# Full-height products for the first block's logits, and two sets of tensors by way of DRAM

## The chip, the cores and the metric

The kernel runs on one core of one Trainium2 chip. The metric is the device time of one launch in microseconds. Of the kernel before, three runs gave 2621.33, 2624.71 and 2629.54 us; their median, 2624.71 us, is the time to compare with.

## What is computed

Two transformer blocks follow each other over 1024 tokens of width 1024, all in float32. The change touches the first half of the first block alone:

```python
h = rmsnorm(x, g_mix[i])
z = h @ w_in[i]
zb, zc, zx, zq, zk, zv = jnp.split(z, ...)
y_c = zb * causal_dwconv3(zc * zx, conv_w[i], conv_b[i])
q = rmsnorm(zq.reshape(b, t, N_HEADS, HEAD_DIM), q_norm_g[i])
k = rmsnorm(zk.reshape(b, t, N_HEADS, HEAD_DIM), k_norm_g[i])
v = zv.reshape(b, t, N_HEADS, HEAD_DIM)
y_a = dilated_attention(q, k, v).reshape(b, t, ATTN_W)
y = jnp.concatenate([rmsnorm(y_c, g_out_conv[i]), rmsnorm(y_a, g_out_attn[i])], axis=-1)
x = x + y @ w_out[i]
```

There are 8 heads of 64 features; `y_c` and `y_a` are 512 wide each. The rest (a gated feed-forward, a second gate, and a second block with sparse attention and retention) is not touched.

## The kernel before

Matrices are stored with features on the 128 partitions and tokens along the free axis. All large buffers are units of 128 x 1024 float32, 51 in all, handed out by `Ctx.take` from the front of a list and put back at its end by `give`; whoever takes a unit waits until its last readers are done. Products are made exact enough by splitting each operand into a high part that TensorE's float32r format holds and a low rest: `mm3` (lines 99 to 101) issues high x high, high x low and low x high into one bank of PSUM.

The first block's mixer is `mixer1`. Attention goes over 4 pairs of heads (`hp` 0 to 3) and, in each, over 8 blocks of 128 queries (`qi`), which makes 32 units of work; unit `qi` has keys up to its own block, 128 (qi + 1) of them. `Attention.run` emits, per unit, the logits of this one, then some steps of a filler, then the values of the unit before. The filler is a generator of dense products that don't depend on attention: the convolution branch (`conv_branch`), the second half of q, k and v, and then the output products (`out_conv`, `out_part`).

- **Logits** (lines 397 and 398). A head's queries stand in `q[e]`: their high part in the 64 rows of this head, their low part in the other 64. The keys' high part stands in both halves of `k[e]`, so one product over 128 rows (line 397) gives high x high plus low x high. The keys' low part of both heads shares one unit `kl`, one head in each half, and the second product (line 398) takes only the 64 rows of its head. Each head has 8 blocks; a block of more than 512 keys takes two chunks, so there are 96 such pairs of products in the first block: 48 over 512 keys, 16 over 384, and 32 over 256 (128 keys are widened to 256).
- **Packing** (`pack_pair`, lines 346 to 364) transposes a pair's keys and queries and splits them; line 361 copies the keys' high part into the other half. `pack_at` says at which `qi` the packing of the next pair begins.
- **After the logits** VectorE adds the bias and takes the minimum (line 400), ScalarE takes the exponential (403), TensorE transposes the weights (417), VectorE and ScalarE copy them back (421, 423), TensorE multiplies with the values (426), and `finish` divides by the sums (505, 506).
- **Norms** (`Norm`). `add` squares a tensor on ScalarE (126 and 129) and adds it on VectorE (130); `rstd` sums over the features with 8 (or 4) one-column products (142), takes the power on VectorE and GpSimd (108, 109), and spreads the result with transposes (145). `one` then scales (157) and splits (93, 94).
- **The convolution's output** is squared as it is made (line 337) and written to DRAM (338); `out_conv` reads it back tile by tile (584), scales, splits, and multiplies with `w_out`.
- **The attention's outputs** `c.ya[hp]` stay in their units until the end; `sums` adds the squares of those that came before it, and the later ones are added in `finish`.

Two orders meet around the change. The program is emitted in the order of the code; then the Tile layer's scheduler (`schedule_with_timeline_sim=True`) moves the instructions of each engine by an estimate of its own. Every engine and every DMA queue then works strictly in its order. Loads and most stores are issued by SP's queue, the convolution's stores by POOL's.

## Time and profile before

| | |
|---|---|
| three runs, median | 2624.71 us |
| the profiled execution | 2630.38 us |
| its span in the profile | 2628.6 us |
| TensorE (PE) busy | 2546.4 us, 97% of the span |
| VectorE (DVE), ScalarE (ACT), GpSimd (POOL) busy | 1721.3, 1120.4, 319.1 us |
| mean granted TensorE clock | 0.977 |

The profile is of one execution. PE is TensorE's matrix products, PEld its weight loads, L99 is line 99 of the kernel. Matrix products overlap: the next one starts before the last has ended, so what one costs in a dense run is the time from its start to the start of the next. A busy row of PE does not say that it works at its best pace. [...]

### The profile page before, as it was taken

How to read it: one execution, taken by the hardware profiler on the slowest of the kernel's cores; microseconds unless marked ns; L12 is line 12 of the kernel's file. 1: busy time of each engine (PE TensorE's matmuls, PEld its weight loads, DVE VectorE, ACT ScalarE, POOL GpSimd, SP SyncE). 2: the span in 40 equal slices, each digit the busy share in tenths (PEclk: the TensorE clock that was granted, in tenths of full speed). 3: DMA queues.
4: the chain of work that ended last, by engine and by line, in shares of the span. 5: the costliest groups of instructions: out<-in, count | busy, mean ns of one | idle time of the engine just before them, and what ended most of it. 6: DMA issues, size and time to landing. Idle time of an engine off the chain costs nothing.

```text
span 2628.6 us, 35665 instructions
## 1 busy us (share of the span) xinstructions
PE 2546.4 (97%) x13706; PEld 2113.9 (80%) x13706; DVE 1721.3 (65%) x3020; ACT 1120.4 (43%) x1913; POOL 319.1 (12%) x299
## 2 busy tenths in 40 slices
PE   8999999998999999999999999989997999999999
PEld 7878887766888887888789989877775888888787
DVE  6443535448877776776766899695658665565854
ACT  5333434234544444334544656543654333333332
POOL 3101101011000000000341233251220000000000
PEclk9999999978999999999999999999998999999999
DMA  6111113111323325644352322321121332227643
GB/s 222 53 41 41 49 49 120 41 65 65 114 106 106 111 104 186 231 159 133 124 183 80 115 91 85 133 89 49 33 77 60 132 117 100 99 99 253 224 154 115
DMA packets 103323, 289.60 MB, mean 110 GB/s; under 512 B 11208, under 2 KB 20464, under 8 KB 103152
## 3 DMA queue, kind: packets, MB, share of 16 engines
q1 hardware_dynamic: 101360, 281.03, 31.3%
q0 software_dynamic: 1792, 6.29, 0.6%
q8 instruction: 107, 1.75, 0.3%
q14 instruction: 64, 0.52, 0.1%
HBM read 211.77 MB, written 75.51 MB: 109 GB/s over the span
## 4 chain that ended last, share of the span: by engine, by line
PE 62%; issue 27%; DVE 7%; DMA 2%; ACT 2%; POOL 1%; SPq 0%; DVEq 0%; POOLq 0%; ACTq 0%
PE m L99 13%; PE m L100 12%; PE m L101 12%; PE m L426 3%; PE m L276 3%; PE m L278 3%; PE m L277 3%; PE m L417 3%; PE m L398 2%; PE m L397 2%; DVE t L94 1%; DVE t L1177 1%; PE m L1459 1%; DVE t L157 1%; PE m L1456 1%
## 5 line engine op out<-in xcount | busy, mean ns | idle before, releaser
L99 PE MATMUL m<-t,t 128*128 128x512 f32 x2520 | 975.1, 397 | 41.0 <-ACT t L93 28.5
L100 PE MATMUL m<-t,t 128*128 128x512 f32 x2520 | 988.1, 393 | 3.3 <-DVE t L94 2.6
L101 PE MATMUL m<-t,t 128*128 128x512 f32 x2520 | 974.1, 392 | 3.0 <-DVE t L94 3.0
L93 ACT ACTIVATE t<-t 128x512 fp32r<-128x512 f32 (+1 forms) x706 | 519.5, 758 | 830.8 <-PE m L100 606.3
L94 DVE TENSOR_TENSOR t<-t,t 128x512 fp32r<-128x512 f32 (+1 forms) x650 | 570.7, 898 | 263.3 <-ACT t L93 251.8
L99 PEld LDWEIGHTS m<-t,t 128*128 128x128 f32 x2520 | 477.9, 190 | 152.6 <-ACT t L93 35.4
L101 PEld LDWEIGHTS m<-t,t 128*128 128x128 f32 x2520 | 476.1, 189 | 103.9 <-DVE t L94 3.7
L100 PEld LDWEIGHTS m<-t,t 128*128 128x128 f32 x2520 | 476.5, 189 | 103.2 <-DVE t L94 4.8
L276 PE MATMUL m<-t,t 128*128 128x256 f32 x896 | 264.6, 296 | 3.1 <-DVE t L1617 2.5
L278 PE MATMUL m<-t,t 128*128 128x256 f32 x896 | 259.6, 290 | 3.7 <-POOL t L94 3.3
L277 PE MATMUL m<-t,t 128*128 128x256 f32 x896 | 259.0, 289 | 0.0
L109 POOL TENSOR_TENSOR rq<-rq,mhalf 128x4 f32<-128x4 f32 (+1 forms) x56 | 79.7, 1424 | 984.1 <-DVE rq L108 967.7
L276 PEld LDWEIGHTS m<-t,t 128*128 128x128 f32 x896 | 176.2, 197 | 9.3 <-DVE t L1617 3.1
L278 PEld LDWEIGHTS m<-t,t 128*128 128x128 f32 x896 | 176.4, 197 | 5.9 <-POOL t L94 3.7
L277 PEld LDWEIGHTS m<-t,t 128*128 128x128 f32 x896 | 176.5, 197 | 1.9 <-issue 1.4
L403 ACT ACTIVATE t<-t,ar 128x256 f32<-128x256 f32 (+7 forms) x128 | 98.9, 773 | 95.1 <-DVE ar L400 92.1
L426 PE MATMUL m<-t,t 128*64 128x128 f32 x1152 | 108.2, 292 | 0.9 <-DVE t L421 0.6
L1174 ACT ACTIVATE t<-t,yss 128x896 f32<-128x896 f32 (+2 forms) x96 | 86.1, 897 | 46.0 <-DVE yss L1187 36.2
L423 ACT ACTIVATE t<-m 128x512 f32<-128x512 f32 (+3 forms) x128 | 56.6, 461 | 109.2 <-PE m L417 108.7
L426 PEld LDWEIGHTS m<-t,t 128*64 128x64 f32 x1152 | 75.7, 143 | 31.6 <-issue 22.3
L400 DVE CUSTOM_DVE_ANT_0 t<-m,t 128x512 f32<-128x512 f32 (+3 forms) x128 | 73.8, 586 | 40.6 <-PE m L398 16.1
L417 PE MATMUL m<-ident,t 128*128 128x128 f32 x576 | 96.1, 289 | 2.7 <-ACT t L1536 1.3
(225 smaller groups left out, 2601.5 us busy)
## 6 DMA issues: line engine op xcount, KB each, us to landing
t<-hd SPq DMA_DIRECT2D x66, 512.0 KB, 3.9
t<-in_w_down_dram SPq DMA_DIRECT2D x66, 512.0 KB, 4.3
t<-in_w_gate_dram SPq DMA_DIRECT2D x48, 512.0 KB, 3.7
t<-in_w_up_dram SPq DMA_DIRECT2D x44, 512.0 KB, 3.7
hd<-t SPq DMA_DIRECT2D x44, 512.0 KB, 2.9
hd<-t SPq DMA_DIRECT2D x66, 256.0 KB, 2.3
t<-in_w_out_dram SPq DMA_DIRECT2D x16, 512.0 KB, 3.6
xf<-t SPq DMA_DIRECT2D x32, 256.0 KB, 2.0
```

The costliest lines, as they stand in the source:

```text
L93: self.nc.scalar.activation(hi.bitcast(F32R), x, AF.Copy)
L94: (eng or self.nc.vector).tensor_tensor(lo.bitcast(F32R), x, hi, OP.subtract)
L99: nc.tensor.matmul(out, w[0], a[0], start=first, stop=False, skip_group_check=skip)
L100: nc.tensor.matmul(out, w[0], a[1], start=False, stop=False, skip_group_check=skip)
L101: nc.tensor.matmul(out, w[1], a[0], start=False, stop=last, skip_group_check=skip)
L276: nc.tensor.matmul(out, ah, wk[0], start=k == 0, stop=False)
L277: nc.tensor.matmul(out, ah, wk[1], start=False, stop=False)
L278: nc.tensor.matmul(out, al, wk[0], start=False, stop=k == NK - 1)
L403: nc.scalar.activation(p[:, :n], p[:, :n], AF.Exp, bias=least, scale=-1.0, accum_out=c.den[:, j:j + 1])
L417: nc.tensor.transpose(tb[:, j * 128:(j + 1) * 128], ps[e][:, (g + j) * 128:(g + j + 1) * 128], c.ident)
L426: nc.tensor.matmul(o[r], self.v(2 * hp + e, kb), ps[e][:, kb * 128:(kb + 1) * 128], start=kb == 0, stop=kb == qi)
L1174: nc.scalar.activation(ja[:, :s.shape[1]], s, AF.Sign, bias=NV[:, j:j + 1], accum_out=ca[:, j:j + 1])
```

## The change

It does five things, all in the first block:

1. The keys' low part gets two units, one per head, and stands in both halves of each, as the high part did. The second logits product then takes all 128 rows, and adds the product of the two low parts, which was left out before.
2. Packing of the next pair begins one unit of work later (`pack_at` 4 for 3).
3. The convolution's squares are no longer taken as its output is made. `out_conv` reads all four tiles back first, squares and adds them there, lets the filler's caller go on once, and then sums over the features.
4. Attention's outputs that are finished before `sums` are also written to DRAM, half by half, on SP's queue; a pair that is complete gives its unit back, and `sums` reads it again. The pairs 0 and 1 go that way; of pair 2 the first half is written too, but not read.
5. The second block's code only loses the row ranges; its products are what they were.

```diff
@@ conv_branch
                 else:
                     nc.vector.tensor_tensor(zc[:, s], b, zc[:, s], OP.mult)
-                    norm.add(zc, h, u)
                     nc.gpsimd.dma_start(c.yc[j][:, s], zc[:, s])
@@ pack_pair
-            if both:
-                nc.vector.tensor_copy(hi[e][ROWS[1 - e], s].bitcast(F32R), hi[e][r, s])
+            for t in (hi[e], lo[e][0]) if both else ():
+                nc.vector.tensor_copy(t[ROWS[1 - e], s].bitcast(F32R), t[r, s])
@@ Attention.logits
-        for e, r in enumerate(self.low_rows):
+        for e in range(2):
...
                 nc.tensor.matmul(b[:, :max(256, m)], q[e][:, t], k[e][:, ch], start=True, stop=False)
-                nc.tensor.matmul(b[:, :max(256, m)], q[e][r, t], kl[r, ch], start=False, stop=True)
+                nc.tensor.matmul(b[:, :max(256, m)], q[e][:, t], kl[e][:, ch], start=False, stop=True)
@@ Attention1
-        self.a, self.ring, self.pack_at = a, ring, 3
+        self.a, self.ring, self.pack_at = a, ring, 4
...
-        self.norm, self.late = Norm(c, 512, c.vec["g_out_attn"], 1e-6), []
+        self.norm, self.late, self.away = Norm(c, 512, c.vec["g_out_attn"], 1e-6), [], []
+        self.yd = [c.dr.tile([128, 1024], F32, name=f"ya{j}") for j in range(4)]
...
-        k, kl = c.takes(2), c.take()
-        yield from pack_pair(c, c.k, hp, c.vec["k_norm_g"], k, [(kl, r) for r in ROWS], self.first if hp == 0 else self.ring, both=True)
+        k, kl = c.takes(2), c.takes(2)
+        yield from pack_pair(c, c.k, hp, c.vec["k_norm_g"], k, list(zip(kl, ROWS)), self.first if hp == 0 else self.ring, both=True)
...
     def sums(self):
 
-        for y, half in self.late:
-            self.norm.add(y, half)
+        for hp in self.away:
+            self.c.ya[hp] = self.c.take()
+            self.c.nc.sync.dma_start(self.c.ya[hp], self.yd[hp])
+        for hp, half in self.late:
+            self.norm.add(self.c.ya[hp], half)
         self.late = None
@@ Attention1.finish
         else:
-            self.late.append((c.ya[hp], half))
+            self.late.append((hp, half))
+            c.nc.sync.dma_start(self.yd[hp][:, s], y)
+            if half:
+                self.away.append(hp)
+                c.give(c.ya[hp])
@@ out_conv
     hi, lo = [], []
+    ys = c.takes(4)
+    for j, yc in enumerate(ys):
+        nc.sync.dma_start(yc, c.yc[j])
+        for h in range(2):
+            n.add(yc, h)
+    yield
     rb = n.rstd((0, 1), ring)
     c.give(n.acc)
-    for j in range(4):
-        yc, p, l = c.takes(3)
+    for j, yc in enumerate(ys):
+        p, l = c.takes(2)
         hi.append(p)
         lo.append(l)
-        nc.sync.dma_start(yc, c.yc[j])
         for h in range(2):
             n.one(yc, j, p, l, h, rb[h], nc.gpsimd if h else nc.vector)
```

The scheduler's order changes between the first packing and the end of the mixer; from the feed-forward on, every engine has the same instructions in the same order as before. Three places matter.

SP's queue, where the convolution's output (`yc`) is read back. Before, two tiles are read ahead of the rest, and tile 0 comes last:

```order
L584 DMA t195_3616<-yc1_385 128x1024
L584 DMA t200_3628<-yc2_386 128x1024
L83 DMA t2_118<-in_w_out_dram 128x1024
L584 DMA t205_3640<-yc3_387 128x1024
L609 DMA t231_4027<-in_xT_dram 128x1024
L487 DMA t62_382<-in_alibi_dram 128x256
L487 DMA t62_382<-in_alibi_dram 128x768
L584 DMA t190_3604<-yc0_384 128x1024
```

With the change tile 0 comes first, tiles 1 and 2 wait until attention's products with the values (line 425) have read the units that they go into, and behind them stand the reloads of attention's outputs (`ya`) and the tiles of x that the output products are added to:

```order
L584 DMA t193_3591<-yc0_384 128x1024
L618 DMA t242_4035<-in_xT_dram 128x1024
L485 DMA t62_382<-in_alibi_dram 128x256
L485 DMA t62_382<-in_alibi_dram 128x768
L618 DMA t243_4066<-in_xT_dram 128x1024
L83 DMA t2_118<-in_w_out_dram 128x1024
L584 DMA t196_3594<-yc3_387 128x1024
L584 DMA t194_3592<-yc1_385 128x1024
L584 DMA t195_3593<-yc2_386 128x1024
L496 DMA t222_3735<-ya0_1001 128x1024
L496 DMA t223_3737<-ya1_1002 128x1024
L618 DMA t228_3754<-in_xT_dram 128x1024
```

PE at the convolution's norm. Before, the sums over the features (L142) stand 9 rows behind the last product of the convolution, and the spreading transposes (L145) are followed by more work of attention:

```order
L397 MATMUL m_130<-t_2307,t_2535 128x512
L398 MATMUL m_130<-t_2308,t_2535 128x512
L142 MATMUL m_127<-ones,t_1430 128x1 x4
L417 MATMUL m_133<-ident,t_3319 128x128 x4
L417 MATMUL m_132<-ident,t_3319 128x128 x2
L426 MATMUL m_134<-t_3318,t_2727 64x128
L142 MATMUL m_127<-ones,t_1430 128x1 x4
```

With the change the sums stand 50 rows behind that product, with 8 transposes of the last unit of pair 2 just ahead, and the spreading transposes stand right before the first triples of the output product:

```order
L416 MATMUL m_133<-ident,t_3573 128x128 x4
L416 MATMUL m_133<-ident,t_3574 128x128 x4
L425 MATMUL m_134<-t_3573,t_2734 64x128
L142 MATMUL m_128<-ones,t_3596 128x1 x8
L425 MATMUL m_134<-t_3574,t_2734 64x128
```

```order
L435 MATMUL m_133<-ident,rd 64x128 x5
L145 MATMUL m_127<-ident,rq 128x128 x4
L145 MATMUL m_128<-ident,rq 128x128 x4
L435 MATMUL m_133<-ident,rd 64x128 x3
L99 MATMUL m_127<-t_3639,t_121 128x512
L100 MATMUL m_127<-t_3640,t_121 128x512
```

PE at the end of attention. Before, the sums of attention's norm for the first half of the tokens are followed by attention alone, and the last ones follow the last division (L436) at once:

```order
L397 MATMUL m_129<-t_3189,t_3445 128x512
L398 MATMUL m_129<-t_3190,t_3445 128x512
L142 MATMUL m_127<-ones,t_3652 128x1 x4
L417 MATMUL m_133<-ident,t_3994 128x128 x4
L426 MATMUL m_134<-t_3993,t_2728 64x128
```

```order
L426 MATMUL m_134<-t_4297,t_2728 64x128
L436 MATMUL m_133<-ident,rd 64x128 x8
L142 MATMUL m_129<-ones,t_3652 128x1 x4
L142 MATMUL m_129<-ones,t_4229 128x1 x4
L145 MATMUL m_130<-ident,rq 128x128 x4
```

With the change two groups of 12 products of the convolution's output stand among the rows behind the first sums (one begins here), and a last group of 12, of attention's output, stands between the division and the last sums (its begin and its end are shown):

```order
L142 MATMUL m_127<-ones,t_3739 128x1 x4
L416 MATMUL m_133<-ident,t_4115 128x128 x4
L416 MATMUL m_132<-ident,t_4115 128x128 x2
L396 MATMUL m_131<-t_3308,t_3563 128x512
L397 MATMUL m_131<-t_3310,t_3563 128x512
L99 MATMUL m_128<-t_3639,t_120 128x512
```

```order
L435 MATMUL m_133<-ident,rd 64x128 x5
L99 MATMUL m_128<-t_4216,t_120 128x512
L100 MATMUL m_128<-t_4220,t_120 128x512
L101 MATMUL m_128<-t_4216,t_124 128x512
```

```order
L101 MATMUL m_128<-t_4219,t_124 128x512
L142 MATMUL m_129<-ones,t_3739 128x1 x4
L142 MATMUL m_129<-ones,t_4268 128x1 x4
L145 MATMUL m_130<-ident,rq 128x128 x4
```

In both, the same products are done; what moved is which of them stand between the steps of a norm.

## Rows read from the trace of the kernel before

**Rows 1.** The page: busy time of the engines

```profile
PE 2546.4 (97%) x13706; PEld 2113.9 (80%) x13706; DVE 1721.3 (65%) x3020; ACT 1120.4 (43%) x1913; POOL 319.1 (12%) x299
```

**Rows 2.** Windows of the mixer: stretch, length, busy by engine (count), PE clock, DMA

```profile
85.00:432.00 347.00, 347.00 (x2226) 283.71 (x2224) 146.88 (x312) 122.34 (x237) 22.44 (x19) 1.00 0.14 49
432.00:456.00 24.00, 22.97 (x133) 16.99 (x133) 15.50 (x30) 13.30 (x25) 5.73 (x5) 0.79 0.64 206
456.00:524.00 68.00, 68.00 (x353) 49.17 (x351) 34.14 (x68) 18.83 (x41) 1.98 (x2) 1.00 0.16 55
524.00:546.00 22.00, 21.68 (x94) 14.26 (x94) 9.44 (x21) 7.68 (x16) 3.69 (x3) 0.53 0.07 23
...
576.00:590.00 14.00, 9.44 (x38) 7.88 (x35) 7.72 (x11) 3.75 (x6) 4.95 (x4) 0.63 0.18 54
```

**Rows 3.** Timeline of PE, first block's attention, 521 to 523.5 us (start, length)

```profile
521.05 0.47 PE L397 MATMUL m<-t,t 128*128 128x512 f32 x1
...
521.88 0.44 PE L397 MATMUL m<-t,t 128*128 128x384 f32 x1
...
522.62 0.50 PE L397 MATMUL m<-t,t 128*128 128x512 f32 x1
...
523.47 1.05 PE L142 MATMUL m<-ones,t 128*128 128x1 f32 x8
```

**Rows 4.** Timeline of PE, second block's attention, 1917.5 to 1919.1 us

```profile
1917.57 0.42 PE L397 MATMUL m<-t,t 128*128 128x384 f32 x1
...
1918.04 0.48 PE L397 MATMUL m<-t,t 128*128 128x512 f32 x1
...
1918.59 0.40 PE L397 MATMUL m<-t,t 128*128 128x512 f32 x1
...
1919.06 0.49 PE L417 MATMUL m<-ident,t 128*128 128x128 f32 x3
```

**Rows 5.** Groups by shape, PE, 130 to 620 us: first block's logits

```profile
L398 PE MATMUL m<-t,t 64*128 64x512 f32 x46 | 24.0, 522 | 0.0
L397 PE MATMUL m<-t,t 128*128 128x512 f32 x46 | 23.3, 507 | 0.0
```

**Rows 6.** The same view, 1768 to 1990 us: second block's logits

```profile
L397 PE MATMUL m<-t,t 128*128 128x512 f32 x37 | 16.8, 455 | 0.0
L398 PE MATMUL m<-t,t 128*128 128x512 f32 x37 | 14.6, 395 | 0.0
```

**Rows 7.** Timeline of all engines at the convolution's norm, 430 to 456 us

```profile
430.56 0.82 PE L417 MATMUL m<-ident,t 128*128 128x128 f32 x6
...
431.75 0.54 POOL L338 DMA_DIRECT2D yc<-t  x1 [5.69 <-DVE t L336]
...
447.49 5.36 DVE L157 SCALAR_TENSOR_TENSOR t<-t,vecs,m 128x512 f32<-128x512 f32 x8 [3.78 <-PE m L145]
447.73 0.60 PE L417 MATMUL m<-ident,t 128*128 128x128 f32 x4
448.26 0.43 PE L426 MATMUL m<-t,t 128*64 128x128 f32 x2
...
452.34 0.47 PE L99 MATMUL m<-t,t 128*128 128x512 f32 x1 [0.36 <-DVE t L157]
```

**Rows 8.** Line 584, the reading back of the convolution's output: time to landing

```profile
DMA to landing us min/median/max: 3.7/4.3/4.4
```

**Rows 9.** Groups by shape, 85 to 590 us: the norms' steps, and the packing's copy

```profile
L109 POOL TENSOR_TENSOR rq<-rq,mhalf 128x8 f32<-128x8 f32 x12 | 19.9, 1661 | 106.9 <-DVE rq L108 106.9
L130 DVE TENSOR_TENSOR t<-t,t 128x512 f32<-128x512 f32 x19 | 13.0, 688 | 6.0 <-ACT t L129 5.7
L129 ACT ACTIVATE t<-t 128x512 f32<-128x512 f32 x19 | 11.9, 628 | 19.0 <-DVE t L616 15.9 <-DVE t L506 3.1
L361 DVE CAST t<-t 64x512 fp32r<-64x512 f32 x14 | 5.9, 422 | 0.4
```

**Rows 10.** Timeline of PE at the end of attention, 579 to 586 us

```profile
579.03 1.85 PE L142 MATMUL m<-ones,t 128*128 128x1 f32 x8 [2.80 <-DVE t L130]
```

More of the change, by code (lines that the diff above doesn't have):

```diff
@@ L313, in qkv_group, with conv_branch @@
     yield from chain((k, 4), (q, 4), (k, 4), (q, 4), (v, 8))
-def conv_branch(c, a, acts, ring, norm):
+def conv_branch(c, a, acts, ring):
     nc = c.nc
@@ L344, with pack_pair @@
 ROWS = (slice(0, 64), slice(64, 128))
-def pack_pair(c, src, hp, gain, hi, lo, ring, both=()):
+def pack_pair(c, src, hp, gain, hi, lo, ring, both=False):
     nc = c.nc
@@ L386, in logits @@
         q, k, kl = self.operands(hp)
-        q, k, kl = [t.bitcast(F32R) for t in q], [t.bitcast(F32R) for t in k], kl.bitcast(F32R)
+        q, k, kl = ([t.bitcast(F32R) for t in ts] for ts in (q, k, kl))
         t = slice(qi * 128, (qi + 1) * 128)
         ps = c.takes(2)
-        for e, r in enumerate(self.low_rows):
+        for e in range(2):
             p, j = ps[e], (2 * hp + e) * 8 + qi
@@ L461 @@
 class Attention1(Attention):
-    low_rows = ROWS
     def __init__(self, c, a, ring):
         super().__init__(c)
-        self.a, self.ring, self.pack_at = a, ring, 3
+        self.a, self.ring, self.pack_at = a, ring, 4
         self.packs = {}
         self.tabs = {}
-        self.norm, self.late = Norm(c, 512, c.vec["g_out_attn"], 1e-6), []
+        self.norm, self.late, self.away = Norm(c, 512, c.vec["g_out_attn"], 1e-6), [], []
+        self.yd = [c.dr.tile([128, 1024], F32, name=f"ya{j}") for j in range(4)]
     def pack(self, hp):
         c = self.c
-        k, kl = c.takes(2), c.take()
-        yield from pack_pair(c, c.k, hp, c.vec["k_norm_g"], k, [(kl, r) for r in ROWS], self.first if hp == 0 else self.ring, both=True)
+        k, kl = c.takes(2), c.takes(2)
+        yield from pack_pair(c, c.k, hp, c.vec["k_norm_g"], k, list(zip(kl, ROWS)), self.first if hp == 0 else self.ring, both=True)
         q = c.takes(2)
@@ L525, in fill @@
         yield from first
-        norm_c = Norm(c, 512, c.vec["g_out_conv"], 1e-6)
-        cv = conv_branch(c, a, acts, ring, norm_c)
+        cv = conv_branch(c, a, acts, ring)
         g1 = qkv_group(c, a, 1, acts, ring)
@@ L534, in fill @@
         c.give(*h)
-        yield from out_conv(c, a, ring, xs, norm_c, at)
+        yield from out_conv(c, a, ring, xs, Norm(c, 512, c.vec["g_out_conv"], 1e-6), at)
         while len(c.ya) < 4:
@@ L1501 @@
 class Attention2(Attention):
-    low_rows = (slice(0, 128), slice(0, 128))
     def __init__(self, c, lat, ring):
@@ L1514, in operands @@
     def operands(self, hp):
-        return self.packs[hp], (self.lat.kh, self.lat.kh), self.lat.kl
+        return self.packs[hp], (self.lat.kh, self.lat.kh), (self.lat.kl, self.lat.kl)
     def bias(self, head, qi, n):
```

## The prediction

> **What bounds the kernel now.** First the engines' shares, to see who works most: PE is busy for 97% of the span, DVE for 65%, ACT for 43% [rows 1]. The change lies in the mixer of the first block alone, so the next view is the mixer cut into stretches [rows 2]. From 85 to 432 us PE has no idle time, DVE works for 146.9 of the 347 us and ACT for 122.3: PE sets the pace, the clock is full, and what PE is spared there the kernel is spared. Then come three stretches in which the clock falls to its lower level for part of the time: 432 to 456 us (mean 0.79), where the convolution's norm is taken; 524 to 546 us (0.53), attention's last units, with little between them; and 576 to 590 us (0.63), where PE is busy for 9.4 of 14 us and waits for the last norm. In the first two PE is hardly idle: 1.0 and 0.3 us.
>
> The third view is PE's timeline, where a product costs the time to the start of the next one. In the first block a pair of logits products over 512 keys takes 0.83 us (521.05 to 521.88) or 0.85 (522.62 to 523.47), one over 384 keys 0.74 [rows 3]. The second block has the same code with 128 rows in both products. There a pair over 512 keys takes 0.55 us behind transposes and 0.47 behind another pair, and one over 384 keys 0.47, with one transpose in it [rows 4]. The clock is full in both. So the experiment that the change makes in the first block already stands in this trace, in the second.
>
> **The logits.** The difference is 0.83 - 0.55 = 0.28 us over 512 keys, and 0.74 - 0.47 = 0.27, or 0.30 less the transpose, over 384. It does not shrink with the columns, so it is a cost per pair, and I take 0.29 for all 96 pairs, the 32 over 256 keys too: **27.7 us less**. The ends: two 512-key pairs that follow each other differ by 0.85 - 0.47 = 0.38, which for the 48 large pairs and 0.29 for the rest makes 32. And the mean lengths of the single products [rows 5, 6], (522 + 507) - (395 + 455) = 179 ns, would make 96 x 0.18 = 17; lengths overlap, so that is the low end and not the value. Nearly three of the four head pairs are done before 432 us, where nothing else holds PE.
>
> [...]
>
> **Packing.** 16 more copies of 64 x 512 on DVE, 0.42 us each [rows 9], are 6.8 us on an engine that is busy for 42% of the stretch; they stand ahead of the queries' packing, so the next pair's logits don't wait for them. Packing begins one unit later and ends in the last unit of a pair, still ahead of the next pair's first logits. I take 0; were its last copies waited for at each of four pairs, 4 x 0.84 = 3.4 us.
>
> **Squares and DRAM.** The 16 squares and their adds are the same in number, only elsewhere. The five stores (256 KB each) and two reloads (512 KB) add 2.3 MB in a stretch whose DMA engines are 14% to 16% busy [rows 2]. Each store waits on SP's queue for `finish`, and the next weight load stands behind it; weights are loaded two ahead, so I take 0 (the fifth rival takes more).
>
> **The convolution's norm** is where the change costs. Before, the sums over the features need only the last square, which stood right behind the convolution. Now they need all four tiles back. Let the last convolution product end at 0. Its store is issued 1.2 us later (430.56 to 431.75 [rows 7]). But what comes last is another tile: the loads of tiles 1 and 2 go into units that attention's next-to-last unit of pair 2 still uses, and PE reaches those readers only after some 19 transposes (0.13 each: 0.53 for 4 [rows 7]), 3 pairs (1.4) and a dozen products with values: about 5 us, 6 with one wait for the packed queries. The load lands 4.3 us later [rows 8], up to 6 as three loads and the bias tables share the engines. Four squares at 0.63 and a last add at 0.69 [rows 9] bring it to 12 to 14 us. PE has work until about 10.5: it waits 2 to 4 us. The power (1.66 [rows 9]) and its neighbours take 2.2 us against 1.5 of work: 0.7. Behind the spreading transposes stand 3 small products and the first 12 triples' products; their last operand needs 7 scalings at 0.67 (5.36 for 8 [rows 7]), a division and 4 splits at 0.69, 8.1 us in all, against 3.3 of work: 4 to 5. Last, the first tile of x stands on SP's queue behind the two reloads, and they behind a split on POOL; DVE, in order, waits for it with attention's minima behind: 2 to 3 us. That is 9 to 13 us of waiting. With it the clock stays low for some 20 us instead of 10 (24 us at 0.79 are 10 at 0.5 [rows 2]), which costs 3 to 5 more where PE has work. Before, the stretch lost 1.0 us idle (0.36 of it ahead of the first triple [rows 7]) and 5 by the clock. So the net is 6 to 12 at face value; since work at half the clock fills some of the waits, I take **7 us more**, between 0 (each wait hides another) and 15 (all at their long ends).
>
> **The end of attention.** From 524 to 546 us PE works at half the clock through attention alone [rows 2]: some 20 us of work that takes 10 at the full clock. Now two groups of the convolution's output product (2.8 us each) stand there, and its logits are shorter and fuller. Where dense products stand the clock was full. I take 6 of the 10 us as gained: **6 us less**, between 0 and 10. And before the last sums PE waits 2.8 us [rows 10]; now 12 products, 2.8 us of work, stand there: **3 us less**, between 0 and 7 (the low clock from 579 us on may go too).
>
> **Sum.** -27.7 + 7 - 6 - 3 = -29.7, and 1 more for waits that I have not found: -28.7. The profiled execution took 2630.4 us: 2601.7. It lies 5.7 above the median of the runs, 2624.7, so I expect **2596 us**. A measurement of this kernel can tell 0.3%, 8 us, from no change.
>
> **The rivals.**
> 1. *Better yet*: the waits at the convolution's norm hide each other and the clock stays up at the end: -28 + 2 - 10 - 6 = -42, 2583 us. For it: PE loses as much at that norm before, without any wait for tiles. Against: the chain of loads is long and PE's order fixed. 14%.
> 2. *Given back*: the norm costs its 15 and the clock at the end falls as before: -25 + 15 - 2 = -12, 2613 us. For it: the low clock comes with sparse work, and a wait makes sparse work. 14%.
> 3. *The height plays no part*: the logits pairs stay at 0.83 and what is left is 7 - 6 - 3: 2623 us. For it: the second block's pairs could be short for another cause, since its heads share one tile of keys. Against: in the rows themselves only the height differs [rows 3, 4]. 5%. [...]
> 4. *It does not do what it says*, because attention is held by its chain through DVE and ACT and not by PE, so that the time appears as waiting: 2620 to 2625 us. Against: no idle PE in 347 us [rows 2]. 3%.
> 5. *Slower*: SP's queue. A store of attention's output that heads the queue holds back the weight loads behind it. It decides once a store waits longer than the load behind it is early; from then on PE waits for weights as long as the division is late, up to half a unit of work, some 7 us (347 us for the 24 units of pairs 0 to 2 [rows 2]), at five stores and two reloads. That is 7 x 7 - 28.7 = +20: 2645 us; slower by over 0.3% from 5.2 us each. No store of this kind stands in the trace; against it, weights are loaded two ahead. 5%.
>
> **How the numbers follow.** My forecast has 59%, 2585 to 2608 us. The range takes in most of rivals 1 and 2: 2580 to 2614. Faster by over 0.3% are the forecast, rival 1 and nearly all of rival 2: 0.86. Within 0.3% are rivals 3 and 4: 0.08. Slower is rival 5 and a bad end of rival 2 together: 0.06.
>
> **What would show it.** The first block's pairs at 0.55 and 0.47 us on PE's timeline, and groups like rows 6 in place of rows 5; the convolution's last product some 20 us earlier than 430.6; at that norm, PE waiting for an add (L130) ahead of its sums, for a split ahead of the first triple, and for DVE ahead of attention's products; a mean clock well over 0.53 in the last 20 us of attention; under 1 us of idle ahead of the last sums. The feed-forward and the second block should take what they take now. It is wrong if the pairs stay over 0.7 us, if PE sits idle before weights between 150 and 430 us, or if the norm's stretch takes over 40 us.

## The result and the profile after

| | before | after |
|---|---|---|
| median of four runs | 2623.21 us | 2598.16 us |
| lowest to highest | 2621.33 to 2629.54 | 2596.48 to 2601.67 |
| profiled execution, span | 2630.38, 2628.6 | 2596.48, 2594.6 |
| PE busy | 2546.4 us | 2508.7 us |

The ratio is 0.990, its 95% interval 0.9883 to 0.9918: some 25 us faster, as forecast (2596 us, 2580 to 2614). The median hides steps of the sum that were wrong against each other; the comparison below finds them. Of all the runs in this document, one of the kernel before (3715 us, mean clock 0.619) and one of experiment 5 (2861 us, 0.818) ran at a much lower clock than the others, and both are left out of the times and ratios.

The page's first line answers to [rows 1]: PE loses 38 us of busy time with the same 13706 products, and DVE gains the 16 copies.

```profile
PE 2508.7 (97%) x13706; PEld 2105.5 (81%) x13706; DVE 1729.8 (67%) x3036; ACT 1119.7 (43%) x1913; POOL 321.1 (12%) x299
```

The mixer by windows, as in [rows 2] (stretch, length, PE, PEld, DVE, ACT and POOL busy with their counts, PE's clock, DMA share, GB/s): attention up to the convolution's norm, that norm, then attention's end, and the last sums.

```profile
85.00:408.00 323.00, 322.66 (x2215) 280.52 (x2214) 147.51 (x322) 120.27 (x232) 20.84 (x18) 1.00 0.18 59
408.00:443.00 35.00, 25.51 (x182) 19.94 (x181) 20.64 (x38) 17.08 (x36) 7.58 (x5) 0.80 0.44 152
...
510.00:545.00 35.00, 33.69 (x213) 26.25 (x211) 19.79 (x31) 12.03 (x22) 3.69 (x3) 1.00 0.25 90
545.00:552.00 7.00, 5.50 (x20) 4.27 (x20) 5.72 (x7) 2.52 (x4) 3.94 (x3) 0.53 0.30 91
```

Three things are to be seen. The first stretch has 2215 matrix products in 323 us, where 2226 took 347 before, and PE still has no idle time (0.34 us). The norm's stretch is the only one in which PE is idle for long: 25.5 of 35 us busy, where it was 23.0 of 24. And the 22 us at a mean clock of 0.53 at the end of attention are not there: up to 545 us the clock is full (1.00). The clock is given as a share of the full one; where it is low, windows of 1 us read 0.50, from 525 to 544 us before and from 422 to 428 us after.

Where the time came from, on PE's timeline between 388 and 390 us (start, length; the lines have moved up by one, L396 and L397 were L397 and L398):

```profile
388.24 0.49 PE L396 MATMUL m<-t,t 128*128 128x512 f32 x1
388.56 0.40 PE L397 MATMUL m<-t,t 128*128 128x512 f32 x1
388.80 0.34 PE L396 MATMUL m<-t,t 128*128 128x384 f32 x1
...
389.16 0.39 PE L396 MATMUL m<-t,t 128*128 128x512 f32 x1
389.39 0.40 PE L397 MATMUL m<-t,t 128*128 128x512 f32 x1
389.62 0.40 PE L99 MATMUL m<-t,t 128*128 128x512 f32 x1
```

A pair over 512 keys takes 0.56 us behind transposes (388.24 to 388.80, where the next pair starts) and 0.46 behind another pair: the figures of the second block [rows 4], not those of [rows 3]. By shape, 130 to 585 us, against [rows 5, 6]:

```profile
L396 PE MATMUL m<-t,t 128*128 128x512 f32 x46 | 19.7, 427 | 0.0
L397 PE MATMUL m<-t,t 128*128 128x512 f32 x46 | 18.2, 396 | 0.0
```

Where time went: PE's waits from 415 us to the output product of the convolution's half, in the timeline of PE (in brackets PE's idle time ahead of the row and what ended it).

```profile
415.02 1.74 PE L425 MATMUL m<-t,t 128*64 128x128 f32 x26 [0.63 <-ACT t L422]
419.33 0.66 PE L416 MATMUL m<-ident,t 128*128 128x128 f32 x4 [1.99 <-DVE t L420]
...
420.53 2.42 PE L142 MATMUL m<-ones,t 128*128 128x1 f32 x16 [0.18 <-DVE t L130]
...
431.37 0.47 PE L99 MATMUL m<-t,t 128*128 128x512 f32 x1 [1.74 <-ACT t L93]
434.81 0.80 PE L100 MATMUL m<-t,t 128*128 128x512 f32 x1 [2.97 <-DVE t L94]
```

The wait of 1.99 us is put down to a copy of DVE (L420), which looks like attention's own business. The chain of waits over the same stretch (start, length, what) shows what held that copy:

```profile
409.28 1.27 PE m L425 x20
410.55 0.02 SPq L584
...
410.60 5.39 DMA t<-yc
...
416.01 0.64 ACT t L129
...
416.67 1.30 DVE t L130 x2
...
418.59 0.68 DVE t L420
419.27 1.21 DVE t L130 x2
...
420.53 2.42 PE m L142 x16
```

Read upwards: PE's sums wait for the adds of the squares, the squares for a tile of the convolution's result, its load for products of attention (L425) that still read the tile it goes into, until 410.55. The adds that wait for these squares stand on DVE ahead of the copy, and so PE waits for the copy. That is the chain the prediction described. The last product of the convolution started at 404.18, so the load was issued 6.4 us later. The four loads took 5.1 us to land in the median and 6.2 at most, where they took 4.3 and 4.4 before [rows 8]:

```profile
DMA to landing us min/median/max: 3.2/5.1/6.2
```

One wait ends otherwise than the prediction had it. Behind the first group of output products PE waits once more, for 1.27 us, ahead of attention's products with the values at 443.25 us. The chain of waits from 436 to 446 us ends there in a copy of ACT (L422) that stands behind the squares of attention's outputs, which have just been read back (L126, L129):

```profile
440.47 1.04 ACT t L126 x2
...
442.00 1.04 ACT t L129 x2
443.04 0.17 ACT t L422
...
443.25 0.43 PE m L425 x2
```

DVE was idle for 1.93 us ahead of 442.55, for the same squares, and its add of the first tile of x (L625) started at 443.16. That tile had landed at 443.04: the load that the prediction named came almost as late, but it isn't what ended the wait.

Before attention's last sums PE now waits less than in [rows 10]:

```profile
544.10 1.35 PE L142 MATMUL m<-ones,t 128*128 128x1 f32 x8 [1.31 <-DVE t L130]
```

### The profile page after: what moved, and what is told of

Same layout as the page of the kernel before. It is cut to its first block, busy times and chain, and to the rows that moved or that the text cites. A ratio compares the mean times of both kernels' runs of the same rounds, so it can differ in the third digit from the quotient of the medians.

```text
span 2594.6 us, 35681 instructions
## 1 busy us (share of the span) xinstructions
PE 2508.7 (97%) x13706; PEld 2105.5 (81%) x13706; DVE 1729.8 (67%) x3036; ACT 1119.7 (43%) x1913; POOL 321.1 (12%) x299
## 4 chain that ended last, share of the span: by engine, by line
PE 84%; DVE 9%; DMA 2%; issue 2%; ACT 2%; POOL 1%; SPq 0%; DVEq 0%; ACTq 0%; POOLq 0%
PE m L99 21%; PE m L100 21%; PE m L101 21%; PE m L425 3%; PE m L276 3%; PE m L278 3%; PE m L277 3%; PE m L416 2%; DVE t L94 2%; DVE t L1186 1%; PE m L396 1%; PE m L397 1%; DVE t L157 1%; PE m L1468 1%; PE m L435 1%
## 5 line engine op out<-in xcount | busy, mean ns | idle before, releaser
L99 PE MATMUL m<-t,t 128*128 128x512 f32 x2520 | 976.1, 397 | 41.8 <-ACT t L93 29.1
L100 PE MATMUL m<-t,t 128*128 128x512 f32 x2520 | 990.7, 394 | 5.1 <-DVE t L94 5.1
L101 PE MATMUL m<-t,t 128*128 128x512 f32 x2520 | 976.6, 393 | 3.0 <-DVE t L94 3.0
L99 PEld LDWEIGHTS m<-t,t 128*128 128x128 f32 x2520 | 479.3, 190 | 151.6 <-ACT t L93 35.5
L100 PEld LDWEIGHTS m<-t,t 128*128 128x128 f32 x2520 | 478.3, 190 | 106.6 <-DVE t L94 8.7
L101 PEld LDWEIGHTS m<-t,t 128*128 128x128 f32 x2520 | 477.4, 189 | 104.4 <-DVE t L94 3.7
L425 PE MATMUL m<-t,t 128*64 128x128 f32 x1152 | 106.0, 285 | 2.3 <-ACT t L422 2.2
L425 PEld LDWEIGHTS m<-t,t 128*64 128x64 f32 x1152 | 73.7, 138 | 34.0 <-issue 21.7
L416 PE MATMUL m<-ident,t 128*128 128x128 f32 x576 | 90.5, 279 | 4.9 <-ACT t L422 2.5
L625 DVE TENSOR_TENSOR t<-m,t 128x512 f32<-128x512 f32 x72 | 49.2, 687 | 67.7 <-PE m L101 62.5
```

The costliest lines, as they stand in the source:

```text
L99: nc.tensor.matmul(out, w[0], a[0], start=first, stop=False, skip_group_check=skip)
L100: nc.tensor.matmul(out, w[0], a[1], start=False, stop=False, skip_group_check=skip)
L101: nc.tensor.matmul(out, w[1], a[0], start=False, stop=last, skip_group_check=skip)
L416: nc.tensor.transpose(tb[:, j * 128:(j + 1) * 128], ps[e][:, (g + j) * 128:(g + j + 1) * 128], c.ident)
L425: nc.tensor.matmul(o[r], self.v(2 * hp + e, kb), ps[e][:, kb * 128:(kb + 1) * 128], start=kb == 0, stop=kb == qi)
```

## The experiments

**1. The height taken back.** The changed kernel in all else, with its two tiles of the keys' low part, its order and its detour; only the second product reads 64 rows again.

```
-  nc.tensor.matmul(b, q[e][:, t], kl[e][:, ch], start=False, stop=True)
+  nc.tensor.matmul(b, q[e][r, t], kl[e][r, ch], start=False, stop=True)
```

> The changed kernel in everything but one: the second logits product takes the 64 rows of its head again, from the keys' low part that stands in two units as in the change (the product of the two low parts is left out, as before the change). Theory (the height of the product is worth about 0.3 us per pair): the 96 pairs go back to 0.83, 0.72 and 0.60 us, so 28 to 31 us slower than the changed kernel, 2625 to 2630 us, and the pairs alone explain it; the clock in the last 20 us of attention stays up, because products of the convolution's output still stand among attention's. Rival 1 (rows play no part in a product's cost): 2598 us, pairs at 0.55. Rival 2 (the full height is what keeps the clock up at the end): 38 us slower or more, with the clock low again over the last 20 us of attention.

Measured: 2628.0 us (2622.59 to 2634.96, ten runs); against the kernel before, beside it, 1.0015 (0.9998 to 1.0031). The changed kernel run on the same chip took 2592.8, the four runs of the result 2598.16: one index is worth 30 to 35 us, more than the whole gain. The pairs are back at 0.84 us (389.53 to 390.37; timeline of PE):

```profile
389.53 0.48 PE L396 MATMUL m<-t,t 128*128 128x512 f32 x1
389.94 0.50 PE L398 MATMUL m<-t,t 64*128 64x512 f32 x1
390.37 0.38 PE L396 MATMUL m<-t,t 128*128 128x256 f32 x1
```

PE's waits at the norm are as in the change (2.40, 1.89 and 2.80 us), and the clock at attention's end is full here too (mean 1.00 from 520 to 542 us), though the second products are as short of rows as before. So the fuller logits, one of the two reasons that the prediction gave, are not needed for a full clock there; experiment 8 shows that the other reason, the products that now stand there, is not needed either.

**2. The detour alone.** The kernel before with the squares and outputs by way of DRAM, and its own packing: one tile for the keys' low part, 64 rows, packing from unit 3.

```
-        self.a, self.ring, self.pack_at = a, ring, 4
+        self.a, self.ring, self.pack_at = a, ring, 3
-        k, kl = c.takes(2), c.takes(2)
+        k, kl = c.takes(2), c.take()
```

(as a difference from the change, with the 64-row product of experiment 1).

> The kernel before with the convolution's squares taken from DRAM and attention's outputs by way of DRAM, the low part of the keys shared and the second product over 64 rows as before, packing begun at 3 as before. Theory: the waits at the convolution's norm cost some 9 us of idle PE, the clock there 1 to 2 us more, and the end of attention gives 3 to 13 back if dense products come to stand there: 2615 to 2632 us, nothing like the change. Rival (the units that come free by way of DRAM are where the gain is from): 2605 us or less.

Measured: 2621.44 us (2613.87 to 2626.26, ten runs), 0.9993 of before (0.9977 to 1.0009). No difference that can be told: by the interval the detour gains at most 6 us and costs at most 2.4. PE's idle time at the norm is 6.1 us, against 1.0 before, so the wait is there; from 85 us to the mixer's last spreading transposes it is 8.9 us against the 7.1 of the second profile in experiment 8. The detour is in the change to make room for the two more tiles. No version with only one of its two parts was run.

**3. Both products over 64 rows.** Is it few rows that cost, or going from 128 to 64 and back? This kernel, the change in all else, leaves out the product of the queries' low part with the keys' high part, so that both products of a head read the same 64 rows.

```
-  nc.tensor.matmul(b, q[e][:, t], k[e][:, ch], start=True, stop=False)
-  nc.tensor.matmul(b, q[e][:, t], kl[e][:, ch], start=False, stop=True)
+  nc.tensor.matmul(b, q[e][r, t], k[e][r, ch], start=True, stop=False)
+  nc.tensor.matmul(b, q[e][r, t], kl[e][r, ch], start=False, stop=True)
```

> Like the first, but the first logits product takes the 64 rows of its head too (the product of the queries' low part with the keys' high part is left out). Theory A (a change of height between neighbouring products is what costs, about 0.19 us each way): from the first product of a pair to its second 0.23 us over 512 keys, while the products on either side of a pair, over 128 rows, pay as before; pairs that follow each other pay nothing between them. Theory B (a product over 64 rows is slow by itself): 0.41 us from the first to the second. In total about what the first takes by A, less some us where pairs follow each other; 10 to 20 us more than that by B.

Measured, one run: 2602.32 us. Between two products over 64 rows the second starts 0.23 us behind the first, as between two over 128 rows. Around a change of height two starts come late. The next product, going from 128 rows to 64 or back, starts after 0.32 us, which is 0.09 more (in the kernel before, behind a product over 128 rows, from 197.93 to 198.25 us); and the one behind it after 0.34, which is 0.11 more (the row of L99 below). So a change of height costs 0.20 us, and what stands between two changes costs what it does at 128 rows. In the kernel before every logits product stands between two changes, and its starts, 0.425 and 0.428 us apart, are 0.23 + 0.11 + 0.09. So few rows cost nothing; the change of height costs. (The row of L99 shows the way back: 0.26 us behind a product over 384 keys, which takes 0.18 otherwise, and 0.34 to L100; from L100 to L101 it is 0.23 again.) What neither theory expected stands in the first two rows, on PE's timeline at 394 us:

```profile
394.50 0.51 PE L397 MATMUL m<-t,t 64*128 64x512 f32 x2
394.83 0.40 PE L398 MATMUL m<-t,t 64*128 64x512 f32 x2
395.06 0.33 PE L397 MATMUL m<-t,t 64*128 64x384 f32 x1
395.24 0.34 PE L398 MATMUL m<-t,t 64*128 64x384 f32 x1
395.50 0.50 PE L99 MATMUL m<-t,t 128*128 128x512 f32 x1
395.84 0.40 PE L100 MATMUL m<-t,t 128*128 128x512 f32 x1
396.08 0.39 PE L101 MATMUL m<-t,t 128*128 128x512 f32 x1
```

Each of those two rows is two products, head 0's in rows 0 to 63 and head 1's in rows 64 to 127, and both are over in the time of one: the next product starts 0.23 us behind the second of these rows, and a row of two is 0.51 us long where that of one (L99) is 0.50, so the two start within about 0.01 us of each other. A change of height costs 0.20 us, over two starts. The weight loads don't show this price: in the trace of the kernel before, ahead of the logits at 432 us, a load of 64 rows takes 0.18 us and one of 128 rows 0.19. But that is not the whole price of a product, which is why the third rival falls.

**4. The change once more**, as a mark on the same chip.

> The changed kernel itself, beside the others on one chip: 2596 to 2602 us, 25 us below the kernel before, and a second profile of it, to see which parts of its trace repeat: idle PE of about 10 us at the convolution's norm, low clock of about 14 us there and none in the last 100 us of attention.

Measured: 2592.8 us (2590.4 to 2598.39, four runs), 0.9889 of before (0.9862 to 0.9916). The waits at the norm come again, 2.78, 1.89 and 2.82 us the longest, and the mean clock of the profiled execution is 0.979, as in the change's first profile.

**5. Two heads at once.** If two row halves run at once, a pair of heads can share all its packed tiles, and three products over 64 rows per head take the place of two over 128. The kernel before, with this packing and no detour:

```
+        q, k = c.takes(2), c.takes(2)
+        for src, gain, (hi, lo) in ((c.k, c.vec["k_norm_g"], k), (c.q, c.qg, q)):
+            yield from pack_pair(c, src, hp, gain, [hi, hi], [(lo, r) for r in ROWS], ring)
...
+            for x in range(3):
+                for e, r in enumerate(ROWS):
+                    nc.tensor.matmul(b[e][:, :max(256, m)], q[x == 1][r, t], k[x == 2][r, ch],
+                                     start=x == 0, stop=x == 2)
```

> The kernel before, with its squares, outputs and order as they are, but the heads of a pair share their four packed tiles (queries high and low, keys high and low: head 0 in rows 0 to 63, head 1 in rows 64 to 127) and each head's logits are three products over its own 64 rows (high x high, low x high, high x low), head 0 and head 1 taking turns in two banks. Theory A (a change of height inside a pair costs 0.19 us on either side, one between 64 rows and the neighbours' 128 only 0.09, and two products in different row halves run at the same time, as the run with both products over 64 rows showed): six products over 512 columns take about three slots of 0.22 to 0.25 us and two edges of 0.09, 0.9 us for both heads against 1.67 before and 1.02 in the change. 96 pairs of products become 48 groups; (1.67 - 0.9) x 48 = 37 us less than before, plus 32 copies of 64 x 512 off DVE, which hide; no wait for tiles that come back from DRAM, so the norm stays as before. 2580 to 2592 us, 4 to 15 less than the change. Theory B (they start together only where the columns happen to leave room; six products take turns): 6 x 0.22 + 0.18 = 1.5 us, 8 us less than before: about 2614. Theory C: two banks are asked for at once out of three, so the next group waits for VectorE's minimum and part is given back as waits of 0.2 to 0.5 us ahead of the second group of each unit over 5 to 8 blocks of keys: 2590 to 2600.

Measured: 2606.67 us (2603.7 to 2610.34, five runs), 0.994 of before (0.9916 to 0.9964). That is none of the three theories' times; it lies between B and C. The rows that tell why are shown with the next kernel, which has the same packing and products.

**6. The same in the changed kernel**, with the detour.

> The same packing and products in the changed kernel, whose squares and outputs go by way of DRAM. Theory A: the logits gain what they gain above; against the change, (1.02 - 0.9) x 48 = 6 us less; against the packed version of the kernel before, plus 9 us of waits at the convolution's norm and minus up to 10 where the clock stays up at attention's end: about equal, 2585 to 2595. If the detour has a price of its own that its order does not give back, it is 5 us or more over the other packed version.

Measured: 2614.18 us (2610.97 to 2618.73, ten runs), 0.9962 of before (0.9946 to 0.9978). Where the order keeps the heads together, a group of six products over 512 keys takes 0.89 us from its start to the next product, which is what theory A said. But a change of height also falls on the neighbours, in front and behind. The rows below are such a group, then the same work with the change's four products over 128 rows (`after`), both from the four transposes ahead of the logits to the third product behind them; and then a head's three products by themselves (timelines of PE):

```profile
344.35 0.60 PE L416 MATMUL m<-ident,t 128*128 128x128 f32 x4
344.88 0.96 PE L490 MATMUL m<-t,t 64*128 64x512 f32 x6
345.77 0.50 PE L99 MATMUL m<-t,t 128*128 128x512 f32 x1
...
346.35 0.40 PE L101 MATMUL m<-t,t 128*128 128x512 f32 x1
```

```profile
332.95 0.60 PE L416 MATMUL m<-ident,t 128*128 128x128 f32 x4
...
334.78 0.39 PE L101 MATMUL m<-t,t 128*128 128x512 f32 x1
```

```profile
139.31 0.96 PE L490 MATMUL m<-t,t 64*128 64x512 f32 x3
140.20 0.50 PE L99 MATMUL m<-t,t 128*128 128x512 f32 x1
```

The whole group takes 2.00 us with its neighbours, the change 1.83. So even a whole group between products over 128 rows is no cheaper than the change's; theory A counted two edges of 0.09 us where there are two changes of 0.20. Three products by themselves take 0.89 us, as much as six, where the change takes 0.5 for a head. Of the 48 groups of six, some 19 stand whole in the trace. There are three banks for logits and a group now asks for two; presumably the scheduler that orders the instructions moves the head whose bank is still in use to a later place (no run with more banks was made). The logits take 48.7 us in all without idle time, against 40.6 in the change. In this order the idea loses; whether groups that follow each other without a change of height would gain was not tried. The two versions also weigh the detour in another surrounding: 7.5 us between the medians, with the intervals of the ratios overlapping. (The packing starts one unit later in the second, too.)

**7. Free tiles for the loads.** The change, with one edit: the four tiles that take the convolution's result are taken from the end of the list of free units.

```
-    ys = c.takes(4)
+    ys = [c.take_last() for _ in range(4)]
```

> The change, with one edit: the four tiles into which the convolution's result is read back take units from the end of the list of free ones, so that their loads need not wait for attention's readers of the unit before. Theory A (the first wait at the norm, 2 us ahead of the sums, is the loads' wait for those readers): it goes, the later waits (division ahead of the triples, minima behind the first tile of x) stay: 2 us less than the change, and the idle time ahead of the sums under 0.5 us. Theory B (the loads are late for another cause, their landing time or the bias tables on the same engines): it stays at 2 us, and so does the time. Units taken late are the ones just given, so a load may as well wait for their last readers: then it grows.

Measured: 2589.7 us (2588.36 to 2590.95, four runs), 0.9874 of before (0.9848 to 0.99). Three of the four loads are issued by 404.6 us, where in the change two of these waited until 408.5 and 410.6, and PE's wait of 2 us for the copy is gone (timeline of PE, its waits after 415 us):

```profile
415.82 1.74 PE L425 MATMUL m<-t,t 128*64 128x128 f32 x26 [0.39 <-ACT t L422]
421.54 1.85 PE L425 MATMUL m<-t,t 128*64 128x128 f32 x29 [0.42 <-DVE t L420]
427.00 0.47 PE L99 MATMUL m<-t,t 128*128 128x512 f32 x1 [1.45 <-DVE t L157]
430.21 0.80 PE L100 MATMUL m<-t,t 128*128 128x512 f32 x1 [2.74 <-DVE t L94]
...
439.88 0.50 PE L99 MATMUL m<-t,t 128*128 128x512 f32 x1 [1.69 <-DVE t L625]
```

Theory A holds for that wait, but its idle time of under 0.5 us ahead of the sums did not come: PE is still idle there for 2.4 us (3.7 in the change), since new waits of 1.05 and 0.29 us for attention's minima stand at 412.6 and 413.4 us. The norm's waits taken together are 8.7 us, against 9.7 in the change's first profile and 8.8 in the one of experiment 9. So the waits do not account for the gain. The low clock at the norm lasts 6.8 us here, 13.6 and 10.2 in those two, and before the last sums 3.4, against 6.8 and 3.4; that is worth 5.1 and 1.7 us. The change was not run beside this kernel: 2589.7 us stand against 2592.8 to 2598.65 in the three sets of its runs.

**8. The kernel before once more**, for a second profile.

> The kernel before once more, for a second profile. Theory A (low clock at attention's end, 20 us in the first profile, goes with the order of that kernel): it stands again between 520 and 550 us. Theory B (it comes and goes from run to run, and is the reason for a profiled execution 5.7 us over the median): it is gone or shorter, and the execution is shorter by about half of what is missing, 5 to 10 us.

Measured: 2621.04 us. Theory B: the low clock at attention's end is gone. The same work, shifted by 1.5 us, in a window of this execution (against the row 524 to 546 of [rows 2]; most of the work of those 22 us is done in these 12):

```profile
522.00:534.00 12.00, 11.09 (x74) 7.22 (x75) 7.52 (x16) 6.45 (x14) 2.59 (x3) 1.00 0.01 1
```

The transposes that spread the mixer's last norm start 10.2 us earlier than in the first profile (572.7 against 582.9 us), and that is about the difference between the two executions, 9.3 us. The kernel's own runs show it as well: of ten beside experiment 9, two with a mean clock of 0.974 and 0.975 took 2632.9 and 2633.9 us, the others, 0.978 to 0.983, from 2616.2 to 2623.8.

**9. Free tiles, and the tile of x first.** Experiment 7, and the reloads of attention's output one group later, so that SP's queue loads the first tile of x ahead of them.

```
+    g = out_part(c, a["w_out"][0], pairs(hi, lo), ring, xs, (0, 1), load=a["xT"])
+    next(g)
     at.sums()
-    yield from out_part(c, a["w_out"][0], pairs(hi, lo), ring, xs, (0, 1), load=a["xT"])
+    yield
+    yield from g
```

> The change with two edits: the convolution's tiles are read back into units from the end of the free list (as in the run above, where PE's wait ahead of the sums over the features went from about 2 us to none), and the two reloads of attention's output and its late sums come one group of products later, so that the first tile of x stands ahead of them on SP's queue. Theory A (the wait of 1.7 to 3 us ahead of the output product's second group is DVE's, which waits for that tile of x behind the reloads): it goes or falls under 0.5 us, the wait for the splits of the convolution's operands (2.7 us) stays: 5 to 8 us less than the change run beside it, 2585 to 2590. Theory B (the waits hide each other: whatever is taken away in one place turns up at the next, at the splits or at attention's minima): the idle time between the last convolution product and the second group stays at 8 us or more, and the time within 3 us of the change.

> The change itself on the same chip, as the mark for the version above: 2592 to 2599 us, with about 10 us of idle PE at the convolution's norm.

Measured: 2590.9 us (2585.97 to 2591.43, six runs), the change beside it 2598.65 (2594.44 to 2601.17, six); 0.9875 (0.9854 to 0.9895) and 0.9913 (0.9893 to 0.9932) of before. The runs of the two do not overlap: 7.7 us better than the change. The wait of 1.69 us that experiment 7 had at the add of x is gone, the one for the splits (2.73 us) stays, as theory A had it:

```profile
428.66 0.47 PE L99 MATMUL m<-t,t 128*128 128x512 f32 x1 [1.45 <-DVE t L157]
431.87 0.75 PE L100 MATMUL m<-t,t 128*128 128x512 f32 x1 [2.73 <-DVE t L94]
```

Theory B falls: the norm's waits are 6.9 us and not 8 or more, and the time is not within 3 us of the change. But experiment 7, which still has that wait, took 2589.7 us. So the second edit earned nothing that can be told, and most of the 7.7 us is likely due to experiment 7's one line; that is not shown, since only the two edits together were measured beside the change. The second edit also moves attention's late squares behind a group of products. In experiment 7 the chain of waits behind the row of 439.88 us goes from these squares (436.22 us) by ACT and DVE to the add, which started at 439.13, 0.7 us after the tile of x had landed. So both bear on that row, and this run doesn't tell them apart.

## Why the prediction was right, and which steps were not

The second profile of the kernel before, 2621.04 us, stands near the middle of its runs, as the change's 2596.48 us does among all fourteen of its own (2590.4 to 2601.67), though it is the lowest of the first four. Between these two, 24.6 us, the steps can be measured:

| step | taken | measured |
|---|---|---|
| logits | -27.7 | -31.0 (PE's time from start to start, without idle time: 71.6 to 40.6 us) |
| convolution's norm, PE's waits | +7 with the clock | +8.7 (1.0 to 9.7 us) |
| the same, clock | (in the 7) | +1.7 (low for 10.2, now 13.6 us) |
| attention's end, clock | -6 | 0 (full in both) |
| last sums | -3 | -1.7 (wait 3.05 to 1.31), -1.7 by the clock (low for 10.2, now 6.8) |

- **Logits**: the mechanism was right and the size a little low. At the full clock and without idle time a pair went from 835 to 514 ns over 512 keys, from 708 to 414 over 384 and from 601 to 291 over 256: 48 x 0.321 + 16 x 0.294 + 32 x 0.310 = 30.0 us; the rest of the 31.0 is work that stood at the lower clock. (The prediction's own 96 x 0.29 is 27.8 and not 27.7.) What it left out is that the last change of height also delays the start behind the product that follows a pair: from there to the next it was 338 ns for products over 512 columns and is 233, 165 and 109 for transposes. Over the 51 pairs that no other pair follows that is some 3.5 us more; together 34.5, as experiment 1 has it on one chip (35). Experiment 1 shows the cause, by one index; the third rival (the height plays no part) falls with it.
- **Packing and stores at nothing**: right. PE is idle for 0.34 us from 85 to 408 us, and experiment 2 with the same stores is as fast as before. The fourth and the fifth rival fall with that.
- **The convolution's norm**: right in kind, order and nearly in size. 9 to 13 us of waits were expected, 9.7 came (the rows shown and 0.36, 0.54 and 1.27 us beside them); the 2 to 4 us ahead of the sums were 3.7, the 4 to 5 for the splits 4.7. In place of the 2 to 3 behind the first tile of x stands a wait of 1.3, which ACT's squares of the outputs that were read back ended, with the load of x just ahead of them. The net came to 10.4 (8.7 + 1.7), inside the 6 to 12 at face value; what was taken off for work at half the clock, down to 7, was 3 too much.
- **The end of attention** is the step that failed. "I take 6 of the 10 us as gained" treated a stretch of low clock as a property of the kernel before. It was one of the execution: gone from the second profile of the same kernel, with the same products in the same order. In the first pair of profiles the change did gain these 10 us; that they lie in the change is not shown. Whether it makes such a fall rarer is open: none of its three profiles has one (mean clocks of 0.979, 0.979 and 0.981), nor have experiments 1 and 2 (1.00 from 520 to 542 us), but neither has the second profile of the kernel before.
- **The 5.7 us** by which the profiled execution stood above the median came off as well. But that surplus was this low clock, which alone is worth 10 us in that execution: taken off as a term and again by the median, it was counted twice. Without the term the sum would have been -22.7 on a median of 2624.7, 2602 us. That 2596 came so near 2598 is luck. What the logits gave more (3.3) and the norm cost more (3.4) cancel; what made up for most of the 6 us that were not there are items that the sum did not have, and a median of the kernel before that is 1.5 us lower with its fourth run.
- **Last sums**: as taken in all, but only half by the wait, of which 1.3 us are left where under 1 was expected; the other half by the clock.
- The steps of the table make -24.0 together. Waits at attention's end are 1.5 us shorter, the mixer's other work takes some 2 us less (the 3.5 us behind the pairs are in it) and what lies behind the mixer 2.7 more; the rest of these is assigned to no cause.
- **Rival 1** (better yet) needed the waits to hide each other and 10 us from the clock: the waits did not, the 10 us were no gain. **Rival 2** (given back) expected 15 at the norm: 10.4 came. Its reason, that the low clock comes with sparse work, is not shown: the same work at attention's end stood at 0.53 in one profile of the kernel before and at 1.00 in the other.

What the detour costs in itself stays open within a few us: experiment 2 says nothing that can be told, experiment 1 against before 4 us with an interval from -0.5 to 8, experiments 5 and 6 some 7 or 8. In each the order around it differs.

## What to carry to other kernels

A matrix product's price lies partly in its neighbours: reading doubled rows to keep every product at 128 rows was cheaper here than computing on half as many (1.83 us against 2.00 in experiment 6). Of the 0.20 us of a change of height, 0.11 showed one start later than the step that caused it, so count it over the neighbours on both sides. Before a stretch of low clock is booked as a gain, look at a second profile of the same kernel, or ask whether it is just what sets the profiled execution apart from the median; never book it and scale to the median too. And where PE waits for an engine that is itself in order, follow the chain past the named instruction: the copy that PE waited for stood behind adds that waited for a load, and one line about which tile the load takes removed that wait. Together with one more edit it made the kernel 7.7 us faster, which is more than the waits account for.

## What was not expected of the hardware

- A change between products over 128 and over 64 rows cost 0.20 us each way, at the edge of a run of 64-row products as between single ones; it showed as 0.09 us at the start behind the change and 0.11 at the one after (0.32 and 0.34 us over 512 columns, against 0.23).
- Products over different halves of the rows, in different banks, ran at the same time without being asked to: two in the time of one, 0.23 us from row to row (experiment 3), and six of two heads in a row of 0.96 us, as long as that of three by themselves (experiment 6).
- The granted clock fell to 0.50 for 20.5 us in a stretch in which PE was idle for 0.3 us, in one profiled execution of the kernel before, and stayed full (1.00) over the same work in the other.
